# Context products of a two-layer backbone: both parts of the context rows in one tile, with pooling sums handed out over ticks and the first modulation in four column groups

## The chip, the cores and the metric

The kernel runs on one core of a Trainium2 chip. The metric is device time in microseconds (us), the median of three runs of one program that does the whole computation in one launch. The engines are named as in the profile: PE is TensorE's matmuls and PEld its weight loads, DVE is VectorE, ACT is ScalarE, POOL is GpSimd, and SP is the sync engine, which here only issues transfers.

## The reference, cut to what matters

Two layers act on 512 latent tokens and 256 context tokens of width 2048. All matrix products are in fp32.

```python
shift, scale, gate = split(silu(c) @ w_mod + b_mod, 3)         # and the same with c_ctx for the context
hc = rms_norm(xc) * (1 + scale_c) + shift_c                    # 256 context rows
h  = rms_norm(x)  * (1 + scale)   + shift                      # 512 latent rows
p, pc = h @ w_in, hc @ w_in                                    # width 6656; in layer 1 the context needs k and v alone
A: y = (window mean of p_a - p_a) @ w_pool * silu(gate)        # centred windows 2, 4, 8, 16
B: neighbourhood attention of the latents, which also attend to the context; context attends to itself
C: GLU -> depthwise convolution of 31 taps -> LayerNorm -> swish -> product, * silu(gate)
x  = x + gate * (concat(A, B, C) @ w_out)                      # and xc alike in layer 0
```

After two layers comes a last RMSNorm of the latents.

## The kernel before, in words

**Split products.** Every fp32 operand of a large product is held in two parts of the type fp32r: a high part hi, which ACT makes by a copy (L298, L273), and the rest lo, which DVE makes by a subtraction (L300, L274). `mm3` (L719 to L723) adds three products into one PSUM bank: whi with hhi (L721), whi with hlo (L722) and wlo with hhi (L723). whi and wlo are the two parts of a weight tile of 128x512, which holds four 128x128 weights; hhi and hlo are those of 128 of the normalised rows, turned so that tokens lie along the free dimension. The latent parts are 512 wide and the context parts 256; `new_h` (L489) gives each of the 16 groups k of 128 channels two tiles of its own for each stream, high and low.

**Blocks.** A block (L693) computes 128 output channels: `u` runs over four weight tiles, and in each of these steps PE does twelve latent products (four k, three each) into bank L and, where the context is used, twelve context products into bank C. The context products of a step run one step late (`self.lag`), so that a block's context ends in the first step of the next block. Then `ev(None, C)` moves the bank on, by ACT (a copy, or tanh) and, for gates, by DVE also, which multiplies. Banks L and C come from the tag "g", which has three PSUM banks used in turn. The 48 blocks of layer 0 behind the first four use the context, and so do the 16 blocks for k and v in layer 1. Each step ends with a `tick` (L123), in which whatever was put off with `later(n, f)` is issued; the order on every engine's queue is the order in which this code issues.

**Weights.** SP's queue loads the raw tiles. In the attention branch (B) DVE makes wlo. In branches A and C (L292 to L296) ACT first writes the rounded -raw into wlo, POOL's queue then adds raw to it by an accumulating transfer (`wlo<-raw`, L295), and ACT writes whi. So in those blocks a wlo is issued from POOL's queue, in order with POOL's own work.

**Branches A and C** (`branch_ca`, L741) come first. Block kinds cu1 and cu2 feed the convolution, whose 31 taps run on DVE, three in a tick (L826). `av` (L973) copies its rows into the tile `up`, and once both streams are there, POOL forms the window sums by doubling (L986, L993), corrects the edges (L998, L1001), and DVE forms `po` (L1004), all issued at that one place. `ag`'s evacuation one block later multiplies `po` with w_pool on PE (L1022).

**Branch B** (`branch_b`, L1043): q, k, v and g blocks for eight pairs of heads. `q_ev` (L1107) puts off `q_split` by two ticks, which splits q (L1121: ACT and DVE) and issues four transfers on SP's queue (L1125). k's split follows one tick after its evacuation.

**The start** (`start`, L522). Rows are loaded into the tiles of the high parts, turned on PE and put (L579) into the tiles of the low parts; `modulate` (L613) then overwrites both. The modulation of layer 0 is a product of `cs` (two columns for c and c_ctx, 30 of zeros) with w_mod (`mod_first`, L337): for every pair j, j+1 of k, 16 tiles `wm` of 128x512 are loaded by SP's queue into 27 buffers; `mm(k)` multiplies each in four column groups of the array, one for each 128 columns of wm and all with the same `cs[:, k, :]`, into 32-row strips of the bank "pv" (L353). `row` copies 128x128 of it by DVE (L382), and `mod_columns` turns it on PE (L389). These steps are handed out between the products of the first four blocks (`Multi`, L1557), in proportion by `between` (L663).

Of the kernel before, what the change touches and what calls it, by code (L numbers as in the profile page):

```python
# [20 lines left out]
KT = 16  # L21
NL = 512
# [70 lines left out]
class Kernel:  # L93
# [84 lines left out]
    def setup(self):  # L178
# [11 lines left out]
        self.h_hi, self.h_lo = {}, {}  # L190
# [146 lines left out]
    def mod_first(self, p, j, bufs):  # L337


        nc = self.nc  # L340
# [7 lines left out]
        def mm(k):  # L348
            if k == 0:
                s["ps"] = self.bank("pv")  # L350
            wm = s.pop(k)
            for t in range(4):
                nc.tensor.matmul(s["ps"][32 * t:32 * t + 32, :128], self.cs[:, k, :],  # L353
                                 wm[:, 128 * t:128 * t + 128], start=k == 0, stop=k == KT - 1)

        def row():
            s["ms"] = self.mod_row(p, s["ps"])

        return ([lambda k=k: load(k) for k in range(KT)], [lambda k=k: mm(k) for k in range(KT)],
                [row, lambda: self.mod_columns(0, j, s["ms"], "t")])  # L360
# [24 lines left out]
    def mod_columns(self, l, j, ms, tag):  # L385

        nc = self.nc
        tp = self.bank(tag)
        nc.tensor.transpose(tp[:, 0:128], ms, self.ident)  # L389
# [5 lines left out]
        v = tp[:, 0:128].rearrange("p (q r) -> p q r", r=32)  # L395
# [93 lines left out]
    def new_h(self, k, cx):  # L489
        key = ("c" if cx else "l") + str(k)  # L490
        n = NCX if cx else NL
        self.h_hi[cx, k] = self.ph.tile([128, n], F32R, tag="hi" + key, name="hi" + key)
        self.h_lo[cx, k] = self.ph.tile([128, n], F32R, tag="lo" + key, name="lo" + key)
# [28 lines left out]
    def start(self, p):  # L522
# [4 lines left out]
        loads = deque(w[0] for w in work if w[0])  # L527
# [8 lines left out]
        for c in range(4):  # L536
            for cx, c1 in ((False, c), (True, 2 * c), (True, 2 * c + 1)):
                for tb in (4, 5) if cx else range(4):
                    w = 256 if cx else 512
                    key = ("c" if cx else "l") + str(2 * c1 + tb - 4 if cx else 4 * c1 + tb)  # L540
                    t = self.ph.tile([128, w], F32, tag="hi" + key, name="x" + key)
# [11 lines left out]
        for r in range(2):  # L553
            nc.gpsimd.memset(self.sel[:, r, r:r + 1], 1.0)
        ones = p.tile([128, 128], F32, name="ones")
# [23 lines left out]
        def put(k, cx, src):  # L579
            key = ("c" if cx else "l") + str(k)  # L580
            t = self.ph.tile([128, src.shape[1]], F32, tag="lo" + key, name="xT" + key)
# [45 lines left out]
        def go(n=1):  # L627
            for _ in range(n):
                if work:
                    ld, f, j = work.popleft()  # L630
                    f()
                    if ld:
                        load()
# [5 lines left out]
        go(8)  # L639
# [14 lines left out]
        go(8)  # L654
        go(6)
# [19 lines left out]
    def mod_order(self, p, bufs, modulate):  # L675

        work = deque()
        for j in range(0, KT, 2):
            ld, mm, (row, columns) = self.mod_first(p, j, bufs)
            work.extend((a, b, None) for a, b in zip(ld, mm))  # L680
            work.append((None, row, "row"))
# [7 lines left out]
            work.append((None, finish, j))  # L689
# [3 lines left out]
    def block(self, l, use_ctx, ev):  # L693
# [3 lines left out]
        for u in range(4):  # L697
# [11 lines left out]
            if use_ctx:  # L709
                def lagged(u=u, hi=hi, lo=lo):  # L710
                    for a in range(4):
                        k = 4 * u + a
                        self.mm3(C[:, 0:NCX], hi[:, a], lo[:, a], self.h_hi[True, k], self.h_lo[True, k], k == 0, k == KT - 1)
                    if u == 3:
                        ev(None, C[:, 0:NCX])
# [3 lines left out]
    def mm3(self, ps, whi, wlo, hhi, hlo, start, stop):  # L719
# [3 lines left out]
        mm(ps, wlo, hhi, start=False, stop=stop)  # L723

# [16 lines left out]
    def branch_ca(self, l, p, first):  # L741
# [54 lines left out]
        def cu1(i):  # L796
            def ev(L, C):
# [3 lines left out]
                else:  # L801
                    nc.scalar.activation(out=s["u1"][:, C0:C0 + NCX], in_=C, func=AF.Copy, scale=0.5)
            return ev

        def cu2(i):
            def ev(L, C):
                a, n = (0, NL) if L is not None else (C0, NCX)
                th = tmp("th", 2, NL)
                nc.scalar.activation(out=th[:, 0:n], in_=L if L is not None else C, func=AF.Tanh, scale=0.5)
# [141 lines left out]
        def gate(o, src):  # L951

            n = o.shape[1]
            th = tmp("th", 2, NL)
            nc.scalar.activation(out=th[:, 0:n], in_=src, func=AF.Tanh, scale=0.5)
# [17 lines left out]
        def av(i):  # L973
            w = (2, 4, 8, 16)[i]

            def ev(L, C):
                a, n = (8, NL) if L is not None else (536, NCX)
                nc.scalar.activation(out=up[:, a:a + n], in_=L if L is not None else C, func=AF.Copy)
# [3 lines left out]
                src, lo, hi = up, 0, end + 8  # L982
                add = nc.gpsimd.tensor_tensor
                a0, a1, d = 1, 0, 1
                b = tmp("s0", 1, UP)
                add(out=b[:, 1:hi], in0=up[:, 0:hi - 1], in1=up[:, 1:hi], op=ALU.add)  # L986
# [650 lines left out]
```

## Time and profile before

| | |
|---|---|
| median of 3 runs | 2387.65 us (2385.43 to 2391.61) |
| the profiled execution | 2382.57 us, of which the span 2380.7 us |
| granted TensorE clock over the span | 0.995 |
| HBM | 296.57 MB read, 24.08 MB written |
| transfers | 385.05 MB, mean 162 GB/s |

A row of a timeline gives the start and the duration in us, the engine, the line of the kernel, the operation, output<-inputs, and in brackets how long the engine was idle before it and what ended that. Matmuls overlap in PE's pipeline, so their durations do not add up: the distance between two starts is what one costs. In the groups of instructions the numbers behind the bars are the busy time in us, the mean duration of one in ns, and the idle time of the engine just before them with its releaser. The names hil and lol are the latent parts of h, hic and loc the context parts; wm is a tile of w_mod.

### The profile page before, as it was taken

To read this page: it belongs to the slowest core of one execution; us is meant where nothing else is said; L and a number is where in the kernel's file an instruction comes from. 1 tells how busy PE (TensorE), PEld (TensorE's weight loads), DVE (VectorE), ACT (ScalarE), POOL (GpSimd) and SP (SyncE) were. 2 spreads that over 40 slices of the span, in tenths; PEclk is the share of its full clock that TensorE was granted. 3 is DMA by queue.
4 is the path that set the end of the run, shared out by engine and by line. 5 is a ranking of instruction groups with operands and counts; after the bars stand their busy time and mean duration, and the time that the engine had idled before them with its cause. 6 is when DMAs were issued, how large, how long until landed. Compare 5 with 4: busy or idle time off the path is not lost. (4 is left out here: it accounts for less than half of the span.)

```text
span 2380.7 us, 36982 instructions
## 1 busy us (share of the span) xinstructions
PE 2328.3 (98%) x13732; PEld 1986.6 (83%) x13732; DVE 1553.7 (65%) x2814; ACT 903.7 (38%) x1790; POOL 523.4 (22%) x654
## 2 busy tenths in 40 slices
PE   6999999999999999999999999999999999999998
PEld 4778888888888888888787887878888888888888
DVE  4359984468777777877666386863666666555435
ACT  3233334333433333344522265444333334344323
POOL 1124444122122212211101122451111211010001
PEclk8999999999999999999999999999999999999999
DMA  9968786555355445526765347986555554334633
GB/s 319 343 174 188 163 199 169 141 163 159 93 153 164 111 128 156 163 93 174 235 202 172 124 140 174 209 181 162 147 140 142 149 146 129 102 88 122 203 120 129
DMA packets 377077, 385.05 MB, mean 162 GB/s; under 512 B 24672, under 2 KB 294080, under 8 KB 376768
## 3 DMA queue, kind: packets, MB, share of 16 engines
q1 hardware_dynamic: 339232, 290.92, 41.7%
q0 software_dynamic: 37664, 91.76, 16.9%
q8 instruction: 108, 1.77, 0.3%
q14 instruction: 73, 0.60, 0.1%
HBM read 296.57 MB, written 24.08 MB: 135 GB/s over the span
## 5 line engine op out<-in xcount | busy, mean ns | idle before, releaser
L721 PE MATMUL g<-hil,whi 128*128 128x512 f32 x1600 | 635.7, 397 | 0.0
L723 PE MATMUL g<-hil,wlo 128*128 128x512 f32 x1600 | 625.8, 391 | 8.7 <-DMA wlo<-raw 8.6
L722 PE MATMUL g<-lol,whi 128*128 128x512 f32 x1600 | 626.9, 392 | 0.0
L300 DVE TENSOR_TENSOR wlo<-raw,whi 128x512 fp32r<-128x512 f32 x424 | 307.6, 729 | 186.1 <-ACT whi L298 185.3
L298 ACT ACTIVATE whi<-raw 128x512 fp32r<-128x512 f32 x440 | 272.4, 624 | 376.1 <-PE g L722 133.1
L723 PEld LDWEIGHTS g<-hil,wlo 128*128 128x128 f32 x1600 | 300.8, 188 | 77.3 <-DMA wlo<-raw 11.2
L721 PEld LDWEIGHTS g<-hil,whi 128*128 128x128 f32 x1600 | 301.6, 189 | 58.8 <-issue 5.8
L369 DVE SCALAR_TENSOR_TENSOR mod<-wm,cond,mod 128x512 f32<-128x512 f32 x420 | 328.5, 824 | 31.5 <-DMA wm<-in_w_mod_dram 31.2
L722 PEld LDWEIGHTS g<-lol,whi 128*128 128x128 f32 x1600 | 301.7, 189 | 53.2 <-issue 1.4
L723 PE MATMUL g<-hic,wlo 128*128 128x256 f32 x1024 | 289.8, 283 | 0.0
L722 PE MATMUL g<-loc,whi 128*128 128x256 f32 x1024 | 289.7, 283 | 0.0
L721 PE MATMUL g<-hic,whi 128*128 128x256 f32 x1024 | 288.4, 282 | 0.0
L826 DVE SCALAR_TENSOR_TENSOR acc<-ypad,cols,acc 128x783 f32<-128x783 f32 (+1 forms) x240 | 231.3, 964 | 7.2
L722 PEld LDWEIGHTS g<-loc,whi 128*128 128x128 f32 x1024 | 195.4, 191 | 9.4
L721 PEld LDWEIGHTS g<-hic,whi 128*128 128x128 f32 x1024 | 195.4, 191 | 9.3
L723 PEld LDWEIGHTS g<-hic,wlo 128*128 128x128 f32 x1024 | 195.4, 191 | 0.0
L1213 ACT ACTIVATE e<-e,m 128x512 f32<-128x512 f32 x128 | 92.6, 724 | 248.3 <-DVE m L1211 248.3
L295 POOL DMA_DIRECT2D wlo<-raw x128 | 115.2, 908 | 262.4 <-ACT wlo L294 224.7
L422 POOL DMA_DIRECT2D wm<-in_w_mod_dram x98 | 71.2, 727 | 335.1 <-DVE mod L369 252.7
L294 ACT ACTIVATE wlo<-raw 128x512 fp32r<-128x512 f32 x128 | 80.5, 629 | 129.9 <-PE g L723 125.6
L1437 POOL TENSOR_TENSOR xn<-xn,res 128x512 f32<-128x512 f32 (+1 forms) x34 | 45.5, 1346 | 332.8 <-DVE xn L1433 273.5
L424 POOL DMA_DIRECT2D wm<-in_w_mod_dram x88 | 48.3, 549 | 246.4 <-DVE mod L369 219.5
(321 smaller groups left out, 3799.7 us busy)
## 6 DMA issues: line engine op xcount, KB each, us to landing
raw<-in_w_in_dram SPq DMA_DIRECT2D x416, 256.0 KB, 3.9
wm<-in_w_mod_dram SPq DMA_DIRECT2D x198, 256.0 KB, 5.9
wm<-in_w_mod_dram POOLq DMA_DIRECT2D x186, 256.0 KB, 4.1
raw<-in_w_out_dram SPq DMA_DIRECT2D x160, 256.0 KB, 3.3
wlo<-raw POOLq DMA_DIRECT2D x128, 256.0 KB, 4.3
q<-parts SPq DMA_DIRECT2D x32, 384.0 KB, 8.3
k<-parts SPq DMA_DIRECT2D x64, 192.0 KB, 4.5
raw<-mixd SPq DMA_DIRECT2D x32, 256.0 KB, 3.3
```

What stands on the lines that cost most here:

```text
L294: nc.scalar.activation(out=lo, in_=t, func=AF.Copy, scale=-1.0)
L295: nc.gpsimd.dma_start(out=lo, in_=t, accum_op=ALU.add)
L298: nc.scalar.activation(out=hi, in_=t, func=AF.Copy)
L300: eng.tensor_tensor(out=lo, in0=t, in1=hi.bitcast(F32), op=ALU.subtract)
L369: self.nc.vector.scalar_tensor_tensor(out=a, in0=wm, scalar=w, in1=a, op0=ALU.mult, op1=ALU.add)
L422: self.wm_queue.dma_start(out=t.rearrange("p (s n) -> p s n", s=2), in_=src)
L424: self.wm_queue.dma_start(out=t, in_=rows[:, 2 * D + 512 * j:2 * D + 512 * j + 512])
L721: mm(ps, whi, hhi, start=start, stop=False)
L722: mm(ps, whi, hlo, start=False, stop=False)
L723: mm(ps, wlo, hhi, start=False, stop=stop)
L826: nc.vector.scalar_tensor_tensor(out=acc[i][:, 0:na], in0=y[:, j:j + na], scalar=w, in1=acc[i][:, 0:na], op0=ALU.mult, op1=ALU.add)
L1213: nc.scalar.activation(out=e, in_=e, func=AF.Exp, scale=-1.0, bias=m[:, 0:1], accum_out=m[:, 1:2])
```

## The change: one context tile, a reduction, sums over ticks, four column groups

- `new_h` makes one 128x512 tile `c{k}` for the context, hi in columns 0 to 255 and lo in 256 to 511. In a block the context costs two products for each k where it had three: whi with the whole tile, 512 wide, into the whole bank C, and wlo with hi, 256 wide, into its first half. In all but the first k the wlo product comes first. The second half of the bank then holds whi with lo, and `whole` adds the halves: a `tensor_reduce` on DVE over pairs 256 apart, out of PSUM. It takes the place of ACT's copy for av, k and v; for cu1 and q ACT scales its result, and for cu2, ag, cg and g ACT and DVE read its result in SBUF.
- `Multi` keeps its three products. `start` uses the context tiles by pairs for the rows before and after turning.
- `av`'s sums are put off: at most two sums in the first tick, one in each of the next two, the edges and `po` in the third.
- `q`'s split is one tick earlier than its transfers, not with them.
- `mod_first` multiplies four k at once: each column group has another `cs[:, k, :]` and all 512 columns of its own wm tile. `row` copies the whole bank, half by DVE and half by ACT, and `columns` folds the four strips by four products with `fold` (the identity's first two columns of each strip, summed) where there was a transpose. Loads follow four at a time.

```diff
+    def whole(self, C, out):
+        if C.shape[1] == NCX:
+            return C
+        self.nc.vector.tensor_reduce(out=out, in_=C.rearrange("p (j n) -> p n j", j=2), axis=AX.X, op=ALU.add)
+        return out
...
         def mm(k):
-            wm = s.pop(k)
-            for t in range(4):
-                nc.tensor.matmul(s["ps"][32 * t:32 * t + 32, :128], self.cs[:, k, :],
-                                 wm[:, 128 * t:128 * t + 128], start=k == 0, stop=k == KT - 1)
+            for g in range(4):
+                nc.tensor.matmul(s["ps"][32 * g:32 * g + 32, :], self.cs[:, k + g, :], s.pop(k + g),
+                                 start=k == 0, stop=k == KT - 4)
         def row():
-            s["ms"] = self.mod_row(p, s["ps"])
+            s["ms"] = p.tile([128, 512], F32, tag="ms", name="ms")
+            nc.vector.tensor_copy(out=s["ms"][:, 0:256], in_=s["ps"][:, 0:256])
+            nc.scalar.activation(out=s["ms"][:, 256:512], in_=s["ps"][:, 256:512], func=AF.Copy)
+        def columns():
+            tp = self.bank("t")
+            for t in range(4):
+                nc.tensor.matmul(tp[:, 2 * t:2 * t + 2], s["ms"][:, 128 * t:128 * t + 128], self.fold,
+                                 start=True, stop=True)
...
     def new_h(self, k, cx):
+        if cx:
+            t = self.h_cx[k] = self.ph.tile([128, 2 * NCX], F32R, tag=f"c{k}", name=f"c{k}")
+            self.h_hi[cx, k], self.h_lo[cx, k] = t[:, 0:NCX], t[:, NCX:]
+            return
...
                 def lagged(u=u, hi=hi, lo=lo):
                     for a in range(4):
                         k = 4 * u + a
-                        self.mm3(C[:, 0:NCX], hi[:, a], lo[:, a], self.h_hi[True, k], self.h_lo[True, k], k == 0, k == KT - 1)
+                        for j in (0, 1) if k == 0 else (1, 0):
+                            o, w, m = ((C, hi, self.h_cx[k]), (C[:, 0:NCX], lo, self.h_hi[True, k]))[j]
+                            nc.tensor.matmul(o, w[:, a], m, start=k == 0 and j == 0, stop=k == KT - 1 and j == 0)
...
# k_ev (v_ev, and av's copy into up, alike)
-                    nc.scalar.activation(out=s["k"][:, NL:NT], in_=C, func=AF.Copy)
+                    self.whole(C, s["k"][:, NL:NT])
...
# q_ev
                 if (C is not None) == cx:
+                    self.later(1, lambda: s.update(qp=parts(s["q"], nt)))
                     self.later(2, q_split)
...
# av, once both streams are in up
+                sums = [first] + [lambda n=n, d=d: wider(n, d) for n, d in ((4, 1), (8, 2), (16, 4)) if w >= n]
+                for n in range(3):
+                    todo = sums[:1] if n else sums[:max(1, len(sums) - 2)]
+                    sums = sums[len(todo):]
+                    for f in todo + [edges] * (n == 2 and not sums):
+                        self.later(n + 1, f)
```

How the order moves, at three places. First PE's queue in layer 0's first block with context behind Multi: two k of its context products, before.

```order
L721 MATMUL g<-hic_653,whi 128x256
L722 MATMUL g<-loc_654,whi 128x256
L723 MATMUL g<-hic_653,wlo 128x256
L721 MATMUL g<-hic_659,whi 128x256
L722 MATMUL g<-loc_660,whi 128x256
L723 MATMUL g<-hic_659,wlo 128x256
```

Now, from the same place (k = 0 to 3; c_595 and so on are the context tiles):

```order
L743 MATMUL g<-c_595,whi 128x512
L743 MATMUL g<-c_595,wlo 128x256
L743 MATMUL g<-c_600,wlo 128x256
L743 MATMUL g<-c_600,whi 128x512
L743 MATMUL g<-c_697,wlo 128x256
L743 MATMUL g<-c_697,whi 128x512
L743 MATMUL g<-c_702,wlo 128x256
L743 MATMUL g<-c_702,whi 128x512
```

Three products for each k became two, and wide and narrow ones now take turns. Second, POOL's queue at the third av (window 8) of layer 0, before; bt and bw are tables built by transfers of POOL's queue.

```order
L986 TENSOR_TENSOR s_3519<-up 128x799
L993 TENSOR_TENSOR s_3521<-s_3519 128x797
L993 TENSOR_TENSOR s_3523<-s_3521 128x793
L998 TENSOR_TENSOR s_3523<-s_3523,kc 128x4
L1001 TENSOR_TENSOR s_3523<-s_3523,kc 128x3
L998 TENSOR_TENSOR s_3523<-s_3523,kc 128x4
L1001 TENSOR_TENSOR s_3523<-s_3523,kc 128x3
L789 DMA bt_88<-bw_86 16x16x256
L295 DMA wlo<-raw 128x512
```

Now:

```order
L1030 TENSOR_TENSOR s_3000<-up 128x799
L295 DMA wlo<-raw 128x512
L826 DMA bt_88<-bw_86 16x16x256
L1037 TENSOR_TENSOR s_3037<-s_3000 128x797
L295 DMA wlo<-raw 128x512
L826 DMA bt_88<-bw_86 16x16x256
L1037 TENSOR_TENSOR s_3070<-s_3037 128x793
L1045 TENSOR_TENSOR s_3070<-s_3070,kc 128x4
L1048 TENSOR_TENSOR s_3070<-s_3070,kc 128x3
```

Between the three sums there now stand the weight transfers that stood behind all of them. Third, PE's queue in the start where a pair's modulation ends, before. L353 is the modulation (x4 is one k in four column groups, x8 are two), L389 the transpose of its row, the rest are products of Multi.

```order
L723 MATMUL g<-hil_795,wlo 128x512
L353 MATMUL pv<-wm,cs 32x128 x4
L721 MATMUL s<-hic_801,whi 128x256
L722 MATMUL s<-loc_802,whi 128x256
L723 MATMUL s<-hic_801,wlo 128x256
L721 MATMUL s<-hic_807,whi 128x256
L722 MATMUL s<-loc_808,whi 128x256
L723 MATMUL s<-hic_807,wlo 128x256
L389 MATMUL t<-kc,ms 128x128
L353 MATMUL pv<-wm,cs 32x128 x8
```

Now, from the last of the six context products behind a pair's last group on:

```order
L753 MATMUL t<-c_600,wlo 128x256
L751 MATMUL g<-hil_685,whi 128x512
L752 MATMUL g<-lol_686,whi 128x512
L753 MATMUL g<-hil_685,wlo 128x512
L751 MATMUL g<-hil_691,whi 128x512
L752 MATMUL g<-lol_692,whi 128x512
L753 MATMUL g<-hil_691,wlo 128x512
L364 MATMUL t<-fold,ms 128x2 x4
L751 MATMUL s<-c_697,whi 128x256
```

Four products of the fold stand where one transpose stood, with six latent products more between them and the group that they read. Over a pair the 16 k come in four groups of the queue, each a line of x4 (four k in as many column groups), where they came in eight.

More of the change, by code (lines that the diff above doesn't have):

```diff
@@ L526, in start @@
         work = self.mod_order(p, WB, lambda k, cx: modulate(k, cx))
-        loads = deque(w[0] for w in work if w[0])
+        loads = deque(f for w in work for f in w[0])
         def load(n=1):
@@ L554, in start @@
             nc.gpsimd.memset(self.sel[:, r, r:r + 1], 1.0)
+        self.fold = p.tile([128, 2], F32, name="fold")
+        nc.vector.tensor_reduce(out=self.fold, in_=self.ident.rearrange("p (g q) -> p q g", g=4)[:, 0:2], axis=AX.X,
+                                op=ALU.add)
         ones = p.tile([128, 128], F32, name="ones")
@@ L579, in put @@
         def put(k, cx, src):
-            key = ("c" if cx else "l") + str(k)
-            t = self.ph.tile([128, src.shape[1]], F32, tag="lo" + key, name="xT" + key)
+            if cx:
+                if k % 2 == 0:
+                    xT["two"] = self.ph.tile([128, 512], F32, tag=f"c{8 + k // 2}", name=f"xTc{k}")
+                t = xT["two"][:, 256 * (k % 2):256 * (k % 2) + 256]
+            else:
+                t = self.ph.tile([128, NL], F32, tag=f"lol{k}", name=f"xTl{k}")
             if (k + k // 4) % 2:
@@ L801, in ev @@
                 else:
-                    nc.scalar.activation(out=s["u1"][:, C0:C0 + NCX], in_=C, func=AF.Copy, scale=0.5)
+                    o = s["u1"][:, C0:C0 + NCX]
+                    nc.scalar.activation(out=o, in_=self.whole(C, o), func=AF.Copy, scale=0.5)
             return ev
@@ L808, in ev @@
                 th = tmp("th", 2, NL)
-                nc.scalar.activation(out=th[:, 0:n], in_=L if L is not None else C, func=AF.Tanh, scale=0.5)
+                src = L if L is not None else self.whole(C, th[:, NCX:NL])
+                nc.scalar.activation(out=th[:, 0:n], in_=src, func=AF.Tanh, scale=0.5)
                 y = ypad[i % 2]
@@ L995, in ev @@
[L995 to L1005 removed]
+                st = {}
@@ new lines, in first, with wider @@
+                def first():
+                    st["b"] = tmp("s0", 1, UP)
+                    add(out=st["b"][:, 1:end + 8], in0=up[:, 0:end + 7], in1=up[:, 1:end + 8], op=ALU.add)
+                    st["lo"], st["hi"] = 1, end + 8
+                def wider(n, d):
+                    b = st["b"]
+                    nb = tmp("s1" if n in (4, 16) else "s0", 1, UP)
+                    lo, hi = st["lo"] + d, st["hi"] - d
+                    add(out=nb[:, lo:hi], in0=b[:, lo - d:hi - d], in1=b[:, lo + d:hi + d], op=ALU.add)
+                    st.update(b=nb, lo=lo, hi=hi)
@@ L1119, in q_split @@
         def q_split():
-            o = parts(s["q"], nt)
+            o = s.pop("qp")
             for h in range(2):
```

95 lines of the change are left out of this document (47 added, 48 removed).

## The prediction

> **What bounds the kernel now.** I read the page's busy times first, then the groups of instructions, then stretches of the timeline to get start-to-start distances, then the table of who waited for whom, by stage.
>
> ```profile
> span 2380.7 us, 36982 instructions
> PE 2328.3 (98%) x13732; PEld 1986.6 (83%) x13732; DVE 1553.7 (65%) x2814; ACT 903.7 (38%) x1790; POOL 523.4 (22%) x654
> ```
>
> TensorE (PE) has something in flight for 98% of the span. That alone says little, since its records overlap, so the distance between starts is what counts. One step of a block in layer 0, matmuls of PE (start, duration):
>
> ```profile
> 499.72 0.40 PE L721 MATMUL g<-hil,whi 128*128 128x512 f32 x1
> ...
> 502.46 0.28 PE L721 MATMUL g<-hic,whi 128*128 128x256 f32 x1
> 502.58 0.28 PE L722 MATMUL g<-loc,whi 128*128 128x256 f32 x1
> 502.70 0.28 PE L723 MATMUL g<-hic,wlo 128*128 128x256 f32 x1
> ...
> 503.78 0.28 PE L723 MATMUL g<-hic,wlo 128*128 128x256 f32 x1
> 503.90 0.40 PE L721 MATMUL g<-hil,whi 128*128 128x512 f32 x1
> ```
>
> Twelve 512-wide latent products start within 502.46 - 499.72 = 2.74 us, 0.228 us each, though each is recorded as 0.40. Twelve 256-wide context products take 503.90 - 502.46 = 1.44 us, 0.120 each. Half the columns cost 53% of the time: about 0.012 us of each product does not scale with its width. Nothing waits in between. By stage (us; busy time of PE, PEld, DVE, ACT, POOL):
>
> ```profile
> 165.00:430.00 265.00, 259.42 (x1475) 224.73 (x1474) 211.59 (x267) 99.40 (x183) 119.33 (x149) 1.00 0.77 180
> 430.00:1130.00 700.00, 697.33 (x4364) 621.14 (x4364) 523.01 (x1006) 257.47 (x544) 142.45 (x187) 1.00 0.50 141
> 1650.00:2150.00 500.00, 498.98 (x2831) 431.77 (x2831) 309.13 (x607) 188.91 (x374) 80.82 (x118) 1.00 0.49 132
> ```
>
> The first is layer 0's branches A and C, the second its attention branch, the third layer 1's attention. In all three PE is the bound, at clock 1.00. What PE waits for at all, and in the first stage alone (the last row):
>
> ```profile
> PE g L723 <- DMA wlo<-raw: 8.6, 6, 2.5
> PE pv L353 <- DMA wm<-in_w_mod_dram: 6.7, 9, 2.3
> PE t L1226 <- DVE pl L1230: 1.6, 2, 1.3
> PE g L723 <- DMA wlo<-raw: 5.6, 4, 2.5
> ```
>
> So an instruction less on PE should be time less, unless another engine then falls behind.
>
> **Context products.** How many there are:
>
> ```profile
> L721 PE MATMUL g<-hic,whi 128*128 128x256 f32 x1024 | 288.4, 282 | 0.0
> ```
>
> That is 64 blocks of 16 steps of k. Each k now costs 3 x 0.120 = 0.360 us. Afterwards it is one 512-wide product with whi and one 256-wide with wlo, 0.228 + 0.120 = 0.348. The columns streamed are the same 768; what goes is one instruction's fixed part, 2 x 0.1200 - 0.2283 = 0.0117 us. Times 1024: **-12.0 us**, all on the path. The starts are rounded to 0.01 us over twelve products, which leaves 9.4 to 14.5 us.
> The Trainium skill speaks for less here: its page "TensorE: Matmul & The Clock Gate", section "Back-to-back issue gap", gives a lone warm matmul N/2.4 + 2.5 ns, whose fixed part is a fifth of what these rows show, and by which this term would be an estimated 2.6 us. The trace does not agree (0.228 where the formula has 0.216), and the trace decides.
>
> **The reductions.** Every block's context bank now holds two halves, which VectorE (DVE) adds. The nearest row is a reduction of the same 512 elements out of PSUM; the third row is a ScalarE (ACT) copy of the kind that disappears:
>
> ```profile
> L1273 DVE TENSOR_REDUCE mc<-s 128x2 f32<-128x512 f32 x16 | 11.0, 686 | 5.1 <-PE s L1269 4.9
> L1215 DVE TENSOR_SCALAR e<-e,m 128x512 f32<-128x512 f32 x128 | 62.5, 488 | 4.5
> L1153 ACT ACTIVATE qs<-g 128x256 f32<-128x256 f32 x16 | 6.1, 382 | 21.9 <-PE g L723 21.9
> ```
>
> The new one writes 256 results with a step of 256 between its two inputs, which no row shows; I take 0.69 us (0.49 if it ran like the plain SBUF pass of the second row, twice the first row, 1.4, if the step cost something). DVE gains 64 x 0.69 = 44 us: 16 of them, 11 us, in the first stage, where it had 212 of 265; 32, 22 us, on 523 of 700; 16, 11 us, on 309 of 500. ACT loses 36 copies (k, v and av), 14 us. On the path: a context bank is not written again until the block after next, since "g" turns over three banks, so there are some 12 us (three steps of 2.74 + 1.44) for a reduction in place of a 0.38 us copy. What is queued behind it on DVE are the splits of weights and of probabilities (L300, L1230). In the attention stages PE waited for DVE's splits (L1226 above) only twice. Should three such places each grow by one reduction, that is **+2**, which I take; bounds 0 and 7 (ten places).
>
> **Pooling sums.** GpSimd (POOL) runs all of a group's sums at once, and the DMA that finishes a weight's low part stands behind them; VectorE stands too:
>
> ```profile
> 319.53 1.51 POOL L986 TENSOR_TENSOR s<-up 128x799 f32<-128x799 f32 x1 [3.49 <-ACT up L978]
> 321.12 3.10 POOL L993 TENSOR_TENSOR s<-s 128x797 f32<-128x797 f32 x2
> ...
> 325.98 0.94 POOL L295 DMA_DIRECT2D wlo<-raw  x1
> L1004 DVE SCALAR_TENSOR_TENSOR po<-s,up 128x512 f32<-128x512 f32 x8 | 5.5, 693 | 31.2 <-POOL s L1001 21.8 <-POOL s L998 6.8 <-ACT wlo L294 2.7
> ```
>
> From 319.53 to 325.98 POOL issues no weight's transfer, and PE's longest wait for wlo, 2.5 us, follows. The change hands the sums out over three ticks, one step of about 4.2 us each, with the due wlo transfers between: no piece is longer than two sums, about 3.3 us. Of the 5.6 us waited in this stage I take **-5** (one short wait follows the convolution's sums, which stay); bounds -5.6 and 0. The waits in layer 1 (8.6 - 5.6 = 3.0) I leave. DVE's own waits for the sums (28.6 us in eight places, most of them in this stage) shrink as well, which pays for part of its 11 us here. A new link is that POOL's first sum now waits for a DVE reduction where it waited for ACT.
>
> **q's split** goes to DVE and ACT one tick earlier, its four transfers stay where they were. The sync queue (SP) stood for it, with weight loads queued behind:
>
> ```profile
> SPq L1125 <- DVE parts L274: 29.2, 15, 3.7
> ```
>
> PE waited for no raw load in that stage, so I take 0; the scores that read q come about seven ticks later.
>
> **The start (modulation of layer 0).** Matmuls in 32-column groups between products, before; then a 512-wide fp32 product (two records each) and the only one-column products with a fresh 128x128 weight:
>
> ```profile
> 94.56 0.28 PE L723 MATMUL t<-hic,wlo 128*128 128x256 f32 x1
> 94.77 0.64 PE L353 MATMUL pv<-wm,cs 128*32 128x128 f32 x16
> 95.35 0.50 PE L721 MATMUL s<-hil,whi 128*128 128x512 f32 x1
> 95.68 0.40 PE L722 MATMUL s<-lol,whi 128*128 128x512 f32 x1
> 95.92 0.39 PE L723 MATMUL s<-hil,wlo 128*128 128x512 f32 x1
> ...
> 101.74 0.27 PE L389 MATMUL t<-kc,ms 128*128 128x128 f32 x1
> ...
> 116.43 0.27 PE L389 MATMUL t<-kc,ms 128*128 128x128 f32 x1
> 361.41 1.02 PE L865 MATMUL t<-acc,ones 128*128 128x512 f32 x2
> 362.27 0.60 PE L865 MATMUL t<-ypad,ones 128*128 128x256 f32 x2
> 383.50 1.40 PE L889 MATMUL t<-ones,ypad 128*128 128x1 f32 x12
> 384.76 0.47 PE L721 MATMUL g<-hil,whi 128*128 128x512 f32 x1
> 60.00:135.00 75.00, 75.00 (x893) 53.03 (x896) 25.71 (x58) 15.59 (x27) 10.12 (x8) 0.98 1.09 338
> L389 PE MATMUL t<-kc,ms 128*128 128x128 f32 x8 | 2.3, 294 | 0.5 <-DVE ms L382 0.5
> ```
>
> Two k took 95.35 - 94.77 = 0.58 us for 1024 columns. A 512-wide fp32 product takes 362.27 - 361.41 = 0.86 us, so four k in four column groups at once take 0.86, about 0.21 each, and two k of before 0.43. The rest is the price of a change between the two kinds: 0.15 here, 0.09 at the product before (0.21 for 0.12) and 0.10 at the one behind (0.33, where the next has 0.24), 0.34 together. Eight changes for each pair of columns become four: -1.4 us. Against it, four fold products of two records cost 8 x (384.76 - 383.50)/12 = 0.84 for a transpose of 0.29: +0.55. Net -0.8 a pair. The DMA engines run at 338 GB/s; a pair needs 16 + 2 transfers of 256 KB, 4.7 MB, 14.0 us, where PE takes 14.69 from transpose to transpose, so about 0.8 is also all that can be had: six pairs, -4.8. At the first pair everything waits in line: the last group of four (+0.65), the row copied by DVE and then by ACT (+0.4, a copy of 0.38 more), the fold (+0.55), 1.6 us. I take **-3**, bounds -5 and +2.
>
> **Sum.** -12 + 2 - 5 - 3 = -18 us. The profiled execution took 2382.57 us (span 2380.7 and 1.9 around it), so 2364.6. It lies 5.1 us under the median of the three runs, 2387.65 (2385.43 to 2391.61); the same step from the median gives **2369.6 us**. A measurement of this kernel can tell about 0.3%, 7.2 us, from no change.
>
> **Rivals.**
> - *Only the products pay* (chance 0.15). The sums' waits move to other ticks, and the start is held by its transfers (DMA share 1.09 in 60 to 135). For it: 338 GB/s barely changes all along. Against it: PE had no idle time in that stretch. -12 + 2 = -10: 2377.7.
> - *A narrow product ahead of a wide one is not free* (0.07). All 256-wide ones stood in runs; mixed, the weight load, 191 ns long, might not hide behind 0.120, and 12 ns each time undoes the saving: 2387.65 - 18 + 12 = 2381.6. Against it: a wide product follows a narrow one at 503.90 with no gap.
>
> ```profile
> L721 PEld LDWEIGHTS g<-hic,whi 128*128 128x128 f32 x1024 | 195.4, 191 | 9.3
> ```
>
>   The skill's gap formula above lies between, at 2379.1 by its estimate, since it leaves 9.4 us of the 12 unpaid.
> - *VectorE becomes the bound* (0.06, slower). In 230 to 300 us it is busy 66.84 of 70:
>
> ```profile
> 230.00:300.00 70.00, 69.30 (x406) 60.20 (x405) 66.84 (x73) 22.99 (x42) 33.71 (x45) 1.00 0.76 171
> ```
>
>   Its delay then reaches POOL's sums (the new link), the wlo transfers behind them, and PE. If every reduction fell on the path: 44 - 20 = +24, 2411.7. It is slower than before from 20/0.69 = 29 exposed reductions of 64. Against it: 12 us of slack in banks, and DVE's waiting for POOL, which mostly goes. The Trainium skill takes this side: "VectorE: DVE Perf Modes", section "Rules for kernel authors", calls tensor_reduce the slowest DVE operation and advises to restructure; that here a reduction takes no longer than other passes over 512 elements, 686 ns, weakens it.
> - *The four groups run one after another* (0.02), now that each has its own tile: 32 groups x 3 x 0.86 = +82 us, 2452. Against it: 16 records ended within 0.64 us before, also with their own columns each.
>
> **How the numbers follow.** My own case has 0.70. Its bounds add to 2362.5 at best (-14.5 - 5.6 - 5) and, with the dear ends of the reductions and the pooling sums (-8), to 2379.7; the median's own scatter is about 3 us. With *only the products pay* and the cheaper half of the third case the range is **2361 to 2382**. Faster by over 0.3% (under 2380.5): 0.70 x 0.95 + 0.15 x 0.7 + 0.07 x 0.3 = **0.79**; slower by over 0.3%: 0.06 and 0.02, **0.08**; the rest, **0.13**.
>
> **What would show it.** In the changed profile: a context step of four k in 1.39 us in place of 1.44; 64 new DVE reductions near 0.69 us, DVE busy near 1600; PE's wait for wlo in 165 to 430 gone or under 1 us; four changes a pair in the start, and the end of layer 0's first products about 3 us earlier. I am wrong if a wide product behind a narrow one starts later than 0.120 after it, if PE shows waits for DVE of over 5 us in the attention stages, or if POOL's first sum waits long for DVE.

## The result, and the profile after

The changed kernel took **2403.91 us** (median of 4 runs, 2402.87 to 2406.38), the kernel before 2389.63 us on the same chip (2385.43 to 2392.5): ratio **1.0073, 95% interval 1.006 to 1.0086**. The two medians as they stand are 14.3 us, 0.6%, apart. It is 0.7% slower where 0.8% faster was forecast. Over the whole span the granted clock is not the reason: it was 0.996 in the profiled execution, and 0.995 before. The first rows of its page:

```profile
span 2401.1 us, 33594 instructions
PE 2334.8 (97%) x11996; PEld 1919.2 (80%) x11996; DVE 1611.0 (67%) x2879; ACT 893.4 (37%) x1762; POOL 526.4 (22%) x654
```

PE has 1736 instructions fewer, ACT is 10 us less busy, DVE 57 us more. The context step of four k does what it should (PE's timeline; start, duration):

```profile
506.49 0.28 PE L743 MATMUL g<-c,wlo 128*128 128x256 f32 x1
506.60 0.40 PE L743 MATMUL g<-c,whi 128*128 128x512 f32 x1
...
507.66 0.40 PE L743 MATMUL g<-c,whi 128*128 128x512 f32 x1
507.89 0.40 PE L751 MATMUL g<-hil,whi 128*128 128x512 f32 x1
```

507.89 - 506.49 = 1.40 us, where it was 1.44 and 1.39 was forecast. No narrow product is late in front of a wide one. The reductions, too, take what was forecast (groups of line 759; min, median, max in ns), but see who waits for them (us, times):

```profile
L759 DVE TENSOR_REDUCE qs<-g x40: 680/692/693, 485.2 to 2193.6; 128x256 f32<-128x512 f32 x40
L759 DVE TENSOR_REDUCE th<-g x10: 679/684/692, 197.5 to 459.7; 128x256 f32<-128x512 f32 x10
...
  ACT parts L273: 60.3, 14
  ACT th L996: 42.0, 8
  ACT qs L1170: 29.2, 8
  ACT t L1238: 22.6, 8
  POOL s L1030: 18.0, 4
```

Not PE, but ScalarE and GpSimd. PE waits one link further on. Its waits in layer 0's branches (165 to 430 us, first row) and in layer 0's attention (430 to 1130 us):

```profile
PE g L753 <- DMA wlo<-raw: 7.3, 6, 2.9
PE g L753 <- DVE wlo L300: 7.1, 9, 2.1
PE t L1283 <- DVE e L1272: 5.1, 7, 1.1
PE t L1283 <- DVE pl L1287: 3.8, 5, 1.3
```

The wait for wlo in the branches was to go from 5.6 us to under 1, and is 7.3. The three rows of the attention come to 16 us; before, the waits of the whole stage came to 2.6 us, 1.6 of them for pl.

How a reduction gets from DVE to PE in the branches, on four engines' timelines (what stands in brackets is the idle time ahead of the row, and what ended it):

```profile
246.59 0.40 PE L743 MATMUL g<-c,whi 128*128 128x512 f32 x1
...
247.73 3.17 DVE L865 SCALAR_TENSOR_TENSOR acc<-ypad,cols,acc 128x783 f32<-128x783 f32 x3
250.81 0.68 DVE L759 TENSOR_REDUCE up<-g 128x256 f32<-128x512 f32 x1
251.65 2.17 POOL L1030 TENSOR_TENSOR s<-up 128x799 f32<-128x799 f32 x1 [6.60 <-DVE up L759]
253.76 0.84 POOL L295 DMA_DIRECT2D wlo<-raw  x1
257.11 0.50 PE L753 MATMUL g<-hil,wlo 128*128 128x512 f32 x1 [1.39 <-DMA wlo<-raw]
```

The bank's last product ended at 246.99, but DVE was in other work, last in the convolution's taps; the reduction came at 250.81, 3.8 us later, POOL had stood 6.60 us until then, the weight's transfer stood behind POOL's sum, and PE stood for the transfer. In the attention, DVE's queue in the tick behind q's context products:

```profile
651.65 0.69 DVE L759 TENSOR_REDUCE qs<-g 128x256 f32<-128x512 f32 x1
653.70 0.96 DVE L274 TENSOR_TENSOR parts<-qs,parts 128x768 fp32r<-128x768 f32 x1 [1.36 <-ACT parts L273]
654.58 0.68 DVE L1287 TENSOR_TENSOR pl<-t,ph 128x512 fp32r<-128x512 f32 x1
655.18 0.68 DVE L1268 CUSTOM_DVE_ANT_0 e<-s,bias 128x512 f32<-128x512 f32 x1
```

The same place before, where no reduction stands, and q's parts one tick later:

```profile
648.63 0.43 DVE L1303 TENSOR_TENSOR mix<-t,pvt 64x256 f32<-64x256 f32 x1
649.09 0.69 DVE L1230 TENSOR_TENSOR pl<-t,ph 128x512 fp32r<-128x512 f32 x1
649.70 0.68 DVE L1211 CUSTOM_DVE_ANT_0 e<-s,bias 128x512 f32<-128x512 f32 x1
...
653.80 0.95 DVE L274 TENSOR_TENSOR parts<-qs,parts 128x768 fp32r<-128x768 f32 x1
```

pl followed mix at once (0.46 us from start to start). Now 654.58 - 651.65 = 2.93 us stand between them: the reduction, 1.36 us of standing for two steps of ACT, and q's parts, all ahead of the splits of probabilities and weights that PE needs. Taking the starts of the latent products of both profiles one by one, layer 0's attention is where the changed kernel falls behind: it is level at its beginning and about 20 us late at its end, mostly about two for each head pair, and 5.6 at one place (near 910 us). Layer 1's attention adds nothing.

**Theories.** 1: q's early parts make VectorE stand in the fullest tick of each pair. 2: the reductions themselves; either (order) because ACT and POOL stand behind them in VectorE's queue, or (time) by their 44 us on VectorE. 3: the spread sums or the start.

### The profile page after: what moved, and what is told of

Same layout as the page of the kernel before. It is cut to its first block, busy times and chain, and to the rows that moved or that the text cites. A ratio compares the mean times of both kernels' runs of the same rounds, so it can differ in the third digit from the quotient of the medians.

```text
span 2401.1 us, 33594 instructions
## 1 busy us (share of the span) xinstructions
PE 2334.8 (97%) x11996; PEld 1919.2 (80%) x11996; DVE 1611.0 (67%) x2879; ACT 893.4 (37%) x1762; POOL 526.4 (22%) x654
## 5 line engine op out<-in xcount | busy, mean ns | idle before, releaser
L743 PE MATMUL g<-c,whi 128*128 128x512 f32 x1024 | 375.6, 398 | 0.0
L377 DVE SCALAR_TENSOR_TENSOR mod<-wm,cond,mod 128x512 f32<-128x512 f32 x420 | 337.1, 844 | 22.7 <-DMA wm<-in_w_mod_dram 22.3
L743 PE MATMUL g<-c,wlo 128*128 128x256 f32 x1024 | 277.0, 281 | 0.0
L865 DVE SCALAR_TENSOR_TENSOR acc<-ypad,cols,acc 128x783 f32<-128x783 f32 (+1 forms) x240 | 238.3, 993 | 7.2
L743 PEld LDWEIGHTS g<-c,whi 128*128 128x128 f32 x1024 | 192.8, 188 | 42.4
L743 PEld LDWEIGHTS g<-c,wlo 128*128 128x128 f32 x1024 | 193.8, 189 | 11.9
L1271 DVE RECIPROCAL m<-m 128x1 f32<-128x1 f32 x128 | 21.0, 164 | 113.0 <-ACT e L1270 113.0
L1429 PE MATMUL g<-whi,hil 128*128 128x512 f32 x240 | 94.3, 393 | 2.3 <-DVE g L1239 1.3
```

Source lines behind the costliest of these rows:

```text
L377: self.nc.vector.scalar_tensor_tensor(out=a, in0=wm, scalar=w, in1=a, op0=ALU.mult, op1=ALU.add)
L743: nc.tensor.matmul(o, w[:, a], m, start=k == 0 and j == 0, stop=k == KT - 1 and j == 0)
L865: nc.vector.scalar_tensor_tensor(out=acc[i][:, 0:na], in0=y[:, j:j + na], scalar=w, in1=acc[i][:, 0:na], op0=ALU.mult, op1=ALU.add)
L1429: mm(ps, mhi, whi, start=start, stop=False)
```

## The experiments

All ratios are to the kernel before on the same chip; 0.1% is 2.4 us. A difference of two such ratios is uncertain by some 4 us either way.

**q's parts late again**, in the changed kernel:

```diff
-                    self.later(1, lambda: s.update(qp=parts(s["q"], nt)))
                     self.later(2, q_split)
...
-            o = s.pop("qp")
+            o = parts(s["q"], nt)
```

> The changed kernel with one thing put back: the parts of q are made in the tick of q_split again, one tick later. Theory 1 (the early parts stand on VectorE behind the reduction and ScalarE's scale, in the busiest tick of each head pair, and all that is queued behind them comes about 2.5 us late, eight times): 2384 us, 2380 to 2390, and the ratio to the kernel before at or below 1.000. Theory 2 (it is the reductions' own 0.69 us each on VectorE that makes TensorE wait): 2400 to 2404 us, as the changed kernel. Theory 3 (the spread pooling sums or the start): also 2400 to 2404 us.

2393.72 us, ratio 1.0027 (1.0016 to 1.0037). Of the loss of 0.73%, the early parts made 0.46%, 11 us. The rest of the loss stays, so theory 1 explains about six tenths of it, and the time lies between the ranges of the two theories. The reverse edit, **early parts alone**, in the kernel before:

> The kernel before with the parts of q made one tick earlier and nothing else: no reductions. Theory 1: slower than the kernel before by 10 to 20 us, 2400 to 2410 us; less than in the changed kernel if the reduction ahead of ScalarE's scale lengthens the stand. Theory 2: no difference, 2389 to 2391 us.

2395.88 us, 1.0035 (1.0022 to 1.0049): 8 us lost without any reduction, a little less than theory 1 gave. So the early parts cost time by themselves. But the stand that theory 1 names is not needed for it: in seven of the eight places of this run VectorE goes on to q's parts after 0.03 us, where it stood 1.36 us in the changed kernel. One of the seven:

```profile
649.46 0.96 DVE L274 TENSOR_TENSOR parts<-qs,parts 128x768 fp32r<-128x768 f32 x1
650.45 0.69 DVE L1231 TENSOR_TENSOR pl<-t,ph 128x512 fp32r<-128x512 f32 x1
```

Here the parts are only ahead of pl, and everything behind them in the queue comes later.

**The context tile alone** (tile, wide product, reductions; in the kernel before, all other parts of the diff left off):

> The kernel before with the context tile, the 512-wide product and the 64 reductions, and nothing else: parts of q late, pooling sums at once, the start as before. Theory 1: faster than the kernel before by the products' gain of about 9.6 us less a few us of waits, 2380 to 2386 us. Theory 2: slower than the kernel before by about 10 us, 2396 to 2403 us.

2407.61 us, 1.0092 (1.0077 to 1.0107), more than theory 2 gave. PE's wait for wlo over the whole run, which was 8.6 us:

```profile
PE g L740 <- DMA wlo<-raw: 17.4, 8, 5.0
```

That the sums, still in one piece, hold up the transfers more once POOL stands behind the reduction would explain it, but was not tried apart.

**The start alone**, and **the spread sums alone**, each in the kernel before:

> The kernel before with the start alone changed: four column groups in the first modulation product, the row in two halves. All theories: 2385 to 2391 us. The prediction put the start at -3 us; the difference of the two profiles at the end of the first stage was -1.1 us, by which it would be 2388.5 us.

> The kernel before with the spread pooling sums alone. The prediction: -5 us, 2381 us (-5.6 to 0). By the difference of the profiles at the end of layer 0's branches, where the waits for the split weights did not go: 2384 to 2387 us, no difference.

The start: 2383.6 us, 0.9989 (0.9981 to 0.9998). The sums: 2375.41 us, **0.9956** (0.9944 to 0.9969), twice what was forecast. PE's wait in the branches, with the sums spread:

```profile
PE g L723 <- DMA wlo<-raw: 0.2, 1, 0.2
```

So both gain, theory 3 falls, and the wait for wlo of 7.3 us in the changed kernel is not one that the spreading failed to remove: alone it leaves 0.2 us, and the reductions bring a wait back. By the starts of the latent products this run is 7.2 us ahead of the kernel before at the end of the branches, where the changed kernel is level: there, too, the reductions cost.

**No reductions.** The changed kernel with q's parts late, and only the bank's first half evicted, by ACT, so that the product of whi and lo is made but left out of the result:

```diff
                     if u == 3:
-                        ev(None, C)
+                        ev(None, C[:, 0:NCX])
...
-                    self.whole(C, s["k"][:, NL:NT])
+                    nc.scalar.activation(out=s["k"][:, NL:NT], in_=C, func=AF.Copy)
```

> The changed kernel with q's parts late again (2393.7 us measured) and without the reductions: the 512-wide product is made, but only its first 256 columns are evicted, by ScalarE as in the kernel before. It leaves out the product of whi and the low part of the context rows. Theory 2a (the 64 reductions, by their time on VectorE or by the chain through them, cost what the products save): 2370 to 2377 us, since the products save 9.6 us, the start 2.6 and the spread sums something. Theory 3 (the wide product or the spread sums cost by themselves): 2385 to 2394 us.

2366.97 us, 0.9924 (0.991 to 0.9937), a little better than theory 2a gave. The reductions with all that hangs on them cost 1.0027 - 0.9924 = 1.03%, **24.6 us**. **The other side**, three narrow products with everything else the same:

```diff
-                        for j in (0, 1) if k == 0 else (1, 0):
-                            o, w, m = ((C, hi, self.h_cx[k]), (C[:, 0:NCX], lo, self.h_hi[True, k]))[j]
-                            nc.tensor.matmul(o, w[:, a], m, start=k == 0 and j == 0, stop=k == KT - 1 and j == 0)
+                        self.mm3(C[:, 0:NCX], hi[:, a], lo[:, a], self.h_hi[True, k], self.h_lo[True, k], k == 0, k == KT - 1)
```

> The changed kernel with q's parts late and the context products as before: three 256-wide products, evicted as in the kernel before; the context tile, the new start and the spread sums stay. By the start (-2.6 us) and the spread sums (-10.5 us) measured by themselves: 2371 to 2376 us. It is also the other side of the kernel without reductions (2367 us): the difference of the two is the price of the wide product alone, expected at 9.6 us by the profile, so 2374 to 2377 us.

2374.34 us, **0.9954** (0.9942 to 0.9966). The wide product is worth 0.9954 - 0.9924 = 0.30%, 7 us, with some 4 of uncertainty either way. This version beats both kernels.

**Order or time?** First, q's factor 0.125 moved from behind the reduction to where the parts are made, all reductions kept:

```diff
-                    o = s["q"][:, NL:NT]
-                    nc.scalar.activation(out=o, in_=self.whole(C, o), func=AF.Copy, scale=0.125)
+                    self.whole(C, s["q"][:, NL:NT])
...
-            o = parts(s["q"], nt)
+            o = p.tile([128, 2, NT], F32R, tag="parts", name="parts")
+            nc.scalar.activation(out=o[:, 0, 0:nt], in_=s["q"][:, 0:nt], func=AF.Copy, scale=0.125)
+            nc.vector.scalar_tensor_tensor(out=o[:, 1, 0:nt], in0=s["q"][:, 0:nt], scalar=0.125,
+                                           in1=o[:, 0, 0:nt].bitcast(F32), op0=ALU.mult, op1=ALU.subtract)
```

> The changed kernel with q's parts late again (2393.7 us measured), and q's context columns no longer scaled by ScalarE behind the reduction: the factor 0.125 is applied where the parts are made. All 64 reductions stay. Theory 2b (it is the order that costs: ScalarE stands behind the reduction, and its ph and VectorE's pl come about 1 us late, once per head pair): 6 to 8 us less, 2386 to 2388 us. Theory 2c (it is VectorE's 44 us of reductions, wherever they stand): no difference, 2392 to 2395 us.

2386.41 us, 1.0002 (0.9993 to 1.001): 6 us from eight places. DVE at q's reduction, with the scale behind it (q's parts late), and then without:

```profile
652.23 0.69 DVE L759 TENSOR_REDUCE qs<-g 128x256 f32<-128x512 f32 x1
653.89 0.69 DVE L1286 TENSOR_TENSOR pl<-t,ph 128x512 fp32r<-128x512 f32 x1 [0.97 <-ACT ph L1285]
```

```profile
650.72 0.69 DVE L759 TENSOR_REDUCE qs<-g 128x256 f32<-128x512 f32 x1
651.44 0.69 DVE L1288 TENSOR_TENSOR pl<-t,ph 128x512 fp32r<-128x512 f32 x1
```

The reduction is as long in both; the 0.97 us was ACT, which had stood for the reduction, and whose next step (ph) DVE needs. Seven of the eight places of the run with the scale show this stand, 6.8 us together. Next, **ACT takes one half, DVE adds the other**, for q, k, v, u and up:

```diff
+        self.nc.scalar.activation(out=out, in_=C[:, NCX:2 * NCX], func=AF.Copy, scale=scale)
+        if scale == 1.0:
+            self.nc.vector.tensor_tensor(out=out, in0=C[:, 0:NCX], in1=out, op=ALU.add)
+        else:
+            self.nc.vector.scalar_tensor_tensor(out=out, in0=C[:, 0:NCX], scalar=scale, in1=out, op0=ALU.mult, op1=ALU.add)
```

> The changed kernel with q's parts late again (2393.7 us measured); for q, k, v, u and the pooling rows ScalarE copies one half (scaled where it is scaled) and VectorE adds the other half from the product's bank, instead of the reduction; the 18 tanh inputs keep it. VectorE works about 46 x 0.26 = 12 us less, and ScalarE doesn't stand behind VectorE for q and u. Theory 2b (order): 6 to 10 us less, 2384 to 2388 us. Theory 2c (VectorE's time): about 12/44 of what all reductions cost, 3 to 6 us less, 2388 to 2391 us. If ScalarE's 32 added copies delay what stands behind them: 2392 us or more.

2382.12 us, 0.9982 (0.9974 to 0.9991), 11 us better than with the reductions and better than either expectation, at 0.42 us for each addition:

```profile
L769 DVE TENSOR_TENSOR qs<-g,qs x32: 415/424/426, 498.5 to 2171.0; 128x256 f32<-128x256 f32 x32
```

It speaks for the order, but changes the time as well. **Late readers** kept all reductions and moved their readers:

```diff
+    def soon(self, C, f):
+        if C is not None and C.shape[1] != NCX:
+            self.later(2, f)
+        else:
+            f()
...
-                        self.later(n + 1, f)
+                        self.later(n + 1 + cx, f)
...
-                    self.later(1, k_split)
+                    self.later(2, k_split)
```

> The changed kernel with q's parts late and unscaled (2386.4 us measured), and every step of ScalarE and GpSimd that reads a reduction's result (tanh, the factor 0.5, k's parts, the pooling sums) issued one tick later. All 64 reductions stay, with their 44 us of VectorE. Theory 2b (it is the order: ScalarE and GpSimd stand behind the reduction in VectorE's queue, and the weight splits behind them): 2368 to 2378 us. Theory 2c (it is VectorE's time): 2383 to 2390 us.

2401.2 us, 1.0074 (1.0059 to 1.0089): far outside both expectations. PE's largest wait of that run says why; it stands for k, whose parts I had moved:

```profile
PE s L1348 <- DMA k<-parts: 11.6, 6, 3.5
```

**With k's parts back**, and the last convolution's input at once:

```diff
-                    self.later(2, k_split)
+                    self.later(1, k_split)
...
-                self.soon(C, fin)
+                self.soon(C if i < 3 else None, fin)
```

> The kernel with late readers (2401 us measured) with two of its delays taken back: k's parts one tick after the eviction as before, and the input of the last convolution at once. If those two made its new waits (TensorE on k's transfers 11.6 us, and 6 us at the end of the branches): 2378 to 2386 us. If late readers cost in another way: 2390 us or more.

2388.32 us, 1.001 (1.0002 to 1.0019), between the two expectations. The wait for k is gone, and with it most of the loss; another that late readers had brought stays, at the end of the branches:

```profile
PE t L941 <- DVE mix L1094: 3.3, 1, 3.3
```

Up to there late readers were ahead of the run with q unscaled, by an amount that changes from block to block: the latent product that starts at 344 us in the kernel before comes 1.6 us earlier than in that run, the one at 367 us 6.5 us earlier. The sign is that of the order theory. Then it is lost again, so the whole gains nothing over 2386.4. The same with **halves for q, k and v**:

> The kernel of the run beside it (late readers, k's parts back), and for q, k and v ScalarE copies one half and VectorE adds the other (0.43 us in place of 0.69, 24 times... 32 in all with layer 1's none): 2373 to 2380 us by the order theory. It would be the best form of the wide product so far; it beats the kernel with the start and the spread sums alone (2374 us) only at the low end.

2386.52 us, 0.9998 (0.9988 to 1.0008): missed, and no better than halves alone. Late readers told nothing on order against time, so three runs put a reduction that nobody reads into the kernel without reductions, ahead of the eviction:

```diff
+        self.junk = self.pc.tile([128, 32], F32, name="junk")
...
+                        self.nc.vector.tensor_reduce(out=self.junk, in_=C.rearrange("p (j n) -> p n j", j=16), axis=AX.X, op=ALU.add)
                         ev(None, C[:, 0:NCX])
```

> The kernel without reductions (2367 us measured: the first 256 columns evicted by ScalarE, the product of whi and the context rows' low part left out), with 64 reductions of the same 128 x 512 input put into VectorE's queue at the same places, into a tile that nobody reads (32 sums a row in place of 256). Theory 2c (VectorE's 44 us of reductions cost by their time): 2383 to 2394 us, as with the reductions read. Theory 2b (it costs that ScalarE and GpSimd stand behind them): 2367 to 2373 us.

2390.13 us, 1.0015 (1.0006 to 1.0024): by the expectation, time. But its trace shows that the run doesn't separate the two: ACT's evictions still stood for the dead reductions, since both read the same bank (these are two of eight rows, 248 us in all).

```profile
ACT qs L1193 <- DVE junk L746: 67.2, 16, 5.1
ACT th L998 <- DVE junk L746: 41.7, 8, 10.9
```

So one run reduces a tile of SBUF in its place (time without order), the other 32 columns of the bank (order with little time):

```diff
-                        self.nc.vector.tensor_reduce(out=self.junk, in_=C.rearrange("p (j n) -> p n j", j=16), axis=AX.X, op=ALU.add)
+                        self.nc.vector.tensor_reduce(out=self.junk, in_=self.h_cx[0].bitcast(F32).rearrange("p (j n) -> p n j", j=16), axis=AX.X, op=ALU.add)
```

```diff
-                        self.nc.vector.tensor_reduce(out=self.junk, in_=C.rearrange("p (j n) -> p n j", j=16), axis=AX.X, op=ALU.add)
+                        self.nc.vector.tensor_reduce(out=self.junk[:, 0:8], in_=C[:, 0:32].rearrange("p (j n) -> p n j", j=4), axis=AX.X, op=ALU.add)
```

> The kernel without reductions (2367 us measured; the product of whi and the context rows' low part left out), with 64 reductions of 128 x 512 in VectorE's queue at the same places, but of a tile in SBUF that is long there: they wait for nothing, and no engine waits for them. VectorE's time without the order. If the time alone costs: 2380 to 2390 us. If it costs that ScalarE stands behind them (with the dead reductions of the product's bank ScalarE's evictions still waited for them, 248 us in all, and the kernel took 2390 us): 2367 to 2373 us.

> The same kernel without reductions, with 64 short ones (32 columns of the product's bank, about 0.1 us each) at the same places, behind which ScalarE's evictions stand. The order without VectorE's time. If the order costs: 2380 to 2390 us. If the time alone costs: 2367 to 2371 us.

Time without order: 2378.36 us, 0.9964 (0.9952 to 0.9977). Order with little time: 2373.46 us, 0.9942 (0.9929 to 0.9954). The groups of the two, and two of the rows on who waited in the second (in the first nobody did):

```profile
L746 DVE TENSOR_REDUCE junk<-c x64: 1033/1086/1121, 174.1 to 2167.4; 128x32 f32<-128x512 f32 x64
```

```profile
L746 DVE TENSOR_REDUCE junk<-g x64: 174/192/193, 175.4 to 2164.1; 128x8 f32<-128x32 f32 x64
...
  ACT qs L1193: 58.5, 16
  ACT th L998: 36.4, 8
```

Against the 0.9924 without any:

| 64 reductions that are | VectorE, us | ACT stands for them | cost |
|---|---|---|---|
| long, waited for by nobody | 64 x 1.09 = 70 | no | 0.40%, 9.5 us |
| short, ahead of the eviction | 64 x 0.19 = 12 | 210 us | 0.18%, 4.3 us |
| 0.69 us, ahead of it, unread | 64 x 0.69 = 44 | 248 us | 0.91%, 22 us |
| 0.69 us, read (q's parts late) | 64 x 0.69 = 44 | yes, and POOL | 1.03%, 25 us |

Each difference is uncertain by some 4 us, so the second is hardly clear of zero. In the last three rows VectorE itself also stood 23.5 to 23.9 us ahead of the reductions, until the bank's last product; in the first it did not. With that, its queue was held for about 70, 36, 68 and 68 us: the first and the third row differ little in VectorE's time, and in who waits they differ most. Neither theory holds alone: 70 us of VectorE that nobody waits for cost less than half of what 44 us cost with ACT behind them, and ACT behind a short one costs little. A reduction is dear when it is both long and waited for. That the delay then goes round (DVE holds ACT, ACT's splits hold DVE, and both hold PE) fits the rows at 651 us and q's 0.97 us, but is argued, not measured apart.

## Why the prediction was wrong, point by point

By ratios, each the difference of one run to the next: the start and the sums together -0.46% (0.9954, with three narrow products), the wide product -0.30%, the reductions +1.03%, q's early parts +0.46%. Sum +0.73%, 17 us, where -18 was forecast. That the sum is the measured one proves nothing, since each term is taken from where the last one ends. In another order the shares move: the tile alone cost 0.92%, where these terms give 0.73% for it.

Two of the prediction's own signs of being wrong came: PE waits 16 us for DVE in layer 0's attention, where over 5 was the sign, and POOL's first sums stand 18.0 us for the reductions. The sign on the products did not.

- **q's split, 0: failed.** I priced its transfers and the scores seven ticks on, and not the instructions at the new place. A step of ACT and one of DVE of 0.96 us were put into a tick where DVE had nothing to spare, ahead of pl, and in the changed kernel DVE also stands 1.36 us for ACT's. It cost 11 us there, and 8 in the kernel before, without the stand. That the sync queue had stood for DVE's parts (29.2 us) was no cover, since nobody had waited there.
- **Reductions, +2 (0 to 7): failed, and this is the larger part.** The duration, 0.69, was right. The cover that I named, 12 us until the bank is written again, is that of PE, which indeed hardly waited for a bank. I did not ask who *reads* the result: ACT and POOL, in order, with the weight splits and their transfers queued behind them. Nor did I price the stay in DVE's queue ahead of the reduction, 3.8 us in the rows at 250.81; my own row had DVE at 66.84 of 70 us there. So the term of +2 was 24.6 us, and 22 of them came back with reductions that nobody reads, but that ACT stands for.
- **The rival "VectorE becomes the bound", given 0.06, is the one that came.** Its place (230 to 300 us, POOL's first sum, the wlo transfers, PE) is the chain of rows at 250.81 to 257.11. Its sum works too: slower from 20 us of exposed reductions, and 24.6 made the kernel with late q slower by 0.27%. It lacked the attention, where DVE is busy only three quarters of the stage, and still the fullest tick is late. The argument that held it down, "12 us of slack in banks", was the failed step again.
  The Trainium skill's advice in "VectorE: DVE Perf Modes", section "Rules for kernel authors", to restructure a reduction would have been right here: the added halves gained 11 us. How much of the 11 us comes from its reason, the operation's own slowness, is not shown: an addition took 0.42 us where a reduction took 0.69, but ACT did half of the work and no longer stood for q and u. The prediction's own argument against it was too wide: a reduction takes longer than the pass of 488 ns over 512 elements in its second row.
- **Products, -12: right in mechanism, too large.** The rows give 0.04 us for four k, 10 us over 1024; the two runs 7 (3 to 11). The upper end, 14.5, is out. The Trainium skill's gap formula ("TensorE: Matmul & The Clock Gate", section "Back-to-back issue gap"), by which it would be an estimated 2.6, is too low by the rows, and just outside the runs' interval.
- **Pooling sums, -5 (-5.6 to 0): right in mechanism, too small.** Alone they brought 10.5 us (7.4 to 13.4), and the wait went from 5.6 to 0.2. Between the profiled executions it is 7.2; the one of before lies under its median. Where the gain beyond the wait comes from is open. In the changed kernel the reductions took the place of what they freed: the new link, named and not priced.
- **Start, -3: right**, 2.6 us (0.5 to 4.5). Two transposes, and two folds at the same places, of before and of after:

```profile
72.38 0.27 PE L389 MATMUL t<-kc,ms 128*128 128x128 f32 x1
145.79 0.27 PE L389 MATMUL t<-kc,ms 128*128 128x128 f32 x1
```

```profile
72.94 0.95 PE L364 MATMUL t<-fold,ms 128*128 128x2 f32 x8
143.25 0.95 PE L364 MATMUL t<-fold,ms 128*128 128x2 f32 x8
```

  Five pairs took 73.41 us and take 70.31, 0.62 less each (0.8 forecast); the first is 0.56 late (1.6 forecast).
- **The other rivals**: the four groups do run together (a pair takes 14.06 us), and a narrow product ahead of a wide one is free (506.60 - 506.49 = 0.11).

## What to carry to other kernels

When an eviction moves to another engine, ask who reads its result and what stands behind that reader in its queue; the slack of the bank is only the writer's side. An instruction that is placed earlier is paid for in the tick where it lands, however idle the engine is on average. Of a change in several parts, time the parts alone: here two of them gained 11 us together, and the part that was its subject lost more.

## What the runs showed of the hardware

- A wait of 2 to 3 us can be followed by a lower clock, and need not be. In the changed kernel PE waits 0.58 and then 2.06 us, and the products behind start 0.43 us apart in place of 0.23; the last row is of the stretch (us; busy PE, PEld, DVE, ACT, POOL; granted clock, DMA share, GB/s):

```profile
916.85 0.80 PE L753 MATMUL g<-hil,wlo 128*128 128x512 f32 x1 [2.06 <-DVE wlo L300]
917.44 0.63 PE L751 MATMUL g<-hil,whi 128*128 128x512 f32 x1
917.87 0.63 PE L752 MATMUL g<-lol,whi 128*128 128x512 f32 x1
917.00:924.00 7.00, 7.00 (x21) 5.71 (x22) 6.57 (x11) 0.60 (x1) 2.65 (x4) 0.58 0.82 203
```

  About 5.5 us at a granted clock near a half cost about as much again as the wait; this is the place where the changed kernel falls back 5.6 us. Behind a longer wait of the same profile the products start 0.23 apart at once:

```profile
351.05 0.50 PE L753 MATMUL g<-hil,wlo 128*128 128x512 f32 x1 [2.87 <-DMA wlo<-raw]
351.39 0.39 PE L751 MATMUL g<-hil,whi 128*128 128x512 f32 x1
351.62 0.39 PE L752 MATMUL g<-lol,whi 128*128 128x512 f32 x1
```

  The kernel before has the same behind 2.50 us (at 330 us). With the context tile alone, waits of 5.01, 2.99 and 2.65 us were followed by 0.43 (the granted clock was 0.50 in the 5 us behind the first, 0.66 behind the others). What decides it was not tried.
- Two readers of one bank, on ACT and on DVE, kept their order in the program: ACT stood 248 us in all for reductions whose results nobody read. Whether the chip or only the program's own waits ask for this order is not shown.
- The same reduction of 128 x 512 took 0.69 us from a bank and 1.09 us from a tile in SBUF that PE reads too. What makes the difference was not tried.
